# Hybrid decoder block: value products of four heads or more in one run, rotary sums on GpSimd, weight casts on ScalarE

## The chip, the cores and the metric

The kernel runs on one core of one Trainium2 chip. The metric is the device time of one execution in microseconds (us), the median of several runs. Shorter is better.

## The reference

One decoder layer over 512 tokens of width 1024, in float32. What matters here is its first part:

```python
h = rmsnorm(x, norm_mix_g); proj = h @ w_in                 # one projection for both head groups
# group A (8 heads): rotary queries, latent keys/values, an indexer picks 128 keys per query
index = einsum('bhqs,bqh->bqs', relu(qi @ ki), wi);  sel = top_k(causal(index), 128)
p = softmax(where(sel, s_A * 96**-0.5, -inf));       o_a = (p @ c_kv) @ w_uv
# group B (8 heads): three dilated causal patterns, merged by their softmax denominators
o_b = merge(dilated_attention(rope(q), rope(k), v))
x = x + concat(o_a, o_b) @ w_out
# then: cross-attention to 256 memory tokens, squared-ReLU MLP of width 4096, final RMSNorm
```

The kernel evaluates the dilated merge as one softmax with a bias (the logarithm of how often a key is seen), and the gathered top-k attention as a dense one whose unselected keys get a bias of -1e30.

## The kernel before, in words

**Dense products.** A weight is streamed in units of two K chunks (128 rows x 512 columns each): a DMA on SP's queue into a `wraw` buffer (three of them), a cast to float32r `whi`, and `wlo = wraw - whi` (six buffers each). A product is three matmuls per K chunk: hi x hi, hi x lo, lo x hi (`mm3`, L155). `split_unit` (L123) takes a letter for each unit: `p` casts on ScalarE and subtracts on GpSimd, `v` casts on ScalarE and subtracts on VectorE, capitals cast on VectorE instead.

**Rotary embedding.** `rope` (L256) reads a product from PSUM: four VectorE products with cosine, sine and minus sine (L271), then two VectorE sums (L279) into a token-row tile (`tok`, or `ghi2`/`ghi3` for the indexer's queries). TensorE transposes that tile (`tp<-ident,tok`). The sine half goes to a scratch tile `rb` with two buffers.

**Attention.** `attend` (L378) handles one block of 128 queries and the 8 heads of a group; there are four blocks in each of group B and group A, block b having 128(b+1) keys. Per head (two at once in the small blocks): a score product `sc`; one VectorE instruction (L407) that adds the bias and takes the row's extreme; an exponential on ScalarE with the row's sum (L409); a reciprocal (L410) and a VectorE product that normalises the row (L412); transposes of the 128x128 pieces into `tp`; a copy to `pT` (L420 on VectorE for two thirds of group A, L422 on ScalarE otherwise); then b+1 value products into `pv`, where even heads take PSUM partitions 0 to 63 (the left half of TensorE's columns) and odd heads 64 to 127 (the right half). The outputs of all heads are split into hi (ScalarE) and lo (VectorE) by `split_from` (L198), the left side of the output projection.

**Order.** The program is written as stages (`group_b(0)`, `queries_a(0)`, `top_k(1)`, `group_b(1)`, and so on, ending with four `group_a` blocks and `keys_cross`), and a scheduler then fixes the order of the instructions on each engine's queue; each queue runs strictly in that order. Filler for TensorE during attention are other products: the queries of group A, the cross-attention's keys (`mm<-h,whi`, 128x256), the first ones of the output projection. From the output projection on the order is the one written.

**Memory tokens.** `norm_mem` (L462) loads two tiles of memory rows into the buffers `ghi1` and `glo1`, squares them on ScalarE (L187), scales them on GpSimd (L467) and transposes them.

Of the kernel before, what the change touches and what calls it, by code (L numbers as in the profile page):

```python
# [11 lines left out]
F32 = mybir.dt.float32  # L12
# [5 lines left out]
P = 128  # L18
# [23 lines left out]
CONST_COLS = 512 + 128 + 3 * 128 + 3 * 64  # L42


def shape_constants():
    """Tables that depend on positions alone: group B's log-multiplicity bias, the causal
    bias of a diagonal block, and the rotary cosines and sines."""
# [7 lines left out]
    for d in (64, 32):  # L55
        inv = np.float32(10000.0) ** (-np.arange(0, d, 2, dtype=np.float32) / np.float32(d))
        ang = np.arange(S, dtype=np.float32)[:, None] * inv.astype(np.float32)[None, :]
        for tab in (np.cos(ang), np.sin(ang), -np.sin(ang)):
            tab = tab.astype(np.float32).reshape(NT, P, d // 2).transpose(1, 0, 2)
            cols.append(tab.reshape(P, NT * (d // 2)))  # L60
# [4 lines left out]
def kernel(  # L65
# [40 lines left out]
    def mmul(*a, **k):  # L106
        ins = nc.tensor.matmul(*a, **k)  # L107
        if ordered[0]:
            tc.keep_in_program_order(ins)

# [12 lines left out]
    def split_unit(raw, hi, lo, how="v"):  # L123
        """float32r hi and lo of raw; how names the engines: p the lo on GpSimd, v on VectorE,
        their capitals the hi on VectorE instead of ScalarE."""
# [6 lines left out]
    def load_weight(w, segs, k0, how, between=None):  # L132
        """w [rows, cols] in DRAM; the column segments side by side, K chunks k0..k0+7.
        Returns (hi, lo): lists over the K chunks of [128, ncols] views."""
# [20 lines left out]
    def mm3(dst, a, b, first=True, last=True, ks=None):  # L155
        """dst += sum_k a_k^T b_k, a and b as (hi list, lo list); lo x lo is below float32."""
# [6 lines left out]
    # ---- RMS norms: the gain is applied where the rows are transposed; a row's 1/rms is kept  # L163
    # apart and applied where the row's products come back ----
# [19 lines left out]
    def mean_square(src, junk, n=D, scale=None):  # L184
        """Mean of a row's squares over n columns, as this part of it adds to it."""
# [16 lines left out]
    def transpose_half(rows, g0, his, los, bank=bank_tp):  # L202
        """rows [128 tokens, 4 chunks of 128] -> transposed, times the gain, as hi + lo per chunk."""
# [11 lines left out]
    # =============================== token mixing ===============================  # L215
# [17 lines left out]
    tab64 = [tabs[:, 128 * i:128 + 128 * i].rearrange("p (t f) -> p t f", t=NT) for i in range(3)]  # L233
    tab32 = [tabs[:, 384 + 64 * i:448 + 64 * i].rearrange("p (t f) -> p t f", t=NT) for i in range(3)]
# [21 lines left out]
    def rope(ps, heads, half, tabs, t, dst, dup=None):  # L256
        """ps [128, heads, 2, half] (token rows, before the norm's 1/rms) -> dst like it, rotated
        by the token's position."""
        cos, sin, nsin = (tab[:, t, None, :].to_broadcast([P, heads, half]) for tab in tabs)
        r = r_mix[:, t:t + 1]  # L260
        n = heads * 2 * half
        rb = tmp.tile([P, 512], F32, name=nm("rb"), tag="rb", bufs=2)
        rbv = rb[:, :n].rearrange("p (h c f) -> p h c f", h=heads, c=2)
        if dup is None:
            ra = dst
        else:
            ra = tmp.tile([P, 512], F32, name=nm("ra"), tag="tok", bufs=2)[:, :n].rearrange(
                "p (h c f) -> p h c f", h=heads, c=2)
# [4 lines left out]
        for c in range(2):  # L273
            times(ra[:, :, c, :], ps[:, :, c, :], cos)
        times(rbv[:, :, 0, :], ps[:, :, 1, :], nsin)
        times(rbv[:, :, 1, :], ps[:, :, 0, :], sin)
        if dup is None:
            for c in range(2):
# [564 lines left out]
```

## Time and profile before

| what | value |
|---|---|
| runs (3) | 845.13, 845.95, 847.27 us; median 845.95 |
| the profiled execution, first to last instruction | 843.6 us |
| TensorE (PE) | busy 821.7 us, 97% |
| VectorE (DVE) / ScalarE (ACT) / GpSimd (POOL) | 474.4 / 331.4 / 293.2 us, 56 / 39 / 35% |
| mean granted TensorE clock | 0.992 |

The profiled execution has no time of its own beyond its span of 843.6 us; the median of the runs is 2.35 us above that, which is what lies around the span. The page cuts the span into 40 slices of 21 us and gives each engine's busy share; a busy TensorE is not one at its peak, since the intervals of its matmuls overlap and their ends are modelled. What a kind of matmul costs is read from one start to the next.

### The profile page before, as it was taken

The numbers are of one execution on the slowest core, as the hardware profiler recorded it, in microseconds if no ns is written. First come the engines' busy times: TensorE is split into PE (matmuls) and PEld (weight loads), VectorE is DVE, ScalarE is ACT, GpSimd is POOL, SyncE is SP. The second block draws the span as 40 slices with busy tenths as digits, with TensorE's granted clock in tenths as the row PEclk, the third lists the DMA queues.
The fourth block names the chain that finished last, engine by engine and source line by source line (L and its number), as shares of the span: only waits on it lengthen the run. The fifth ranks groups of instructions, "written<-read, shape, count | busy, mean of one in ns | idle before, by whom it ended". The sixth has DMA issues, their size and how long they took to land.

```text
span 843.6 us, 11086 instructions
## 1 busy us (share of the span) xinstructions
PE 821.7 (97%) x4182; PEld 679.2 (81%) x4182; DVE 474.4 (56%) x1010; ACT 331.4 (39%) x676; POOL 293.2 (35%) x179
## 2 busy tenths in 40 slices
PE   7899999999999999999999999999999999999997
PEld 6788787886787788788898878888888888888886
DVE  7876999998777634535673344423542244225413
ACT  5354424457754524223464433213431243123322
POOL 5734303131513405544501233333333333333351
PEclk9899999999999999999999999999999999999999
DMA  7443122112412303332510223333233322322202
GB/s 278 125 125 88 33 74 70 63 21 80 150 53 99 96 5 100 99 100 86 184 56 19 82 100 101 101 99 100 100 100 99 100 100 97 103 91 85 99 1 100
DMA packets 44516, 77.34 MB, mean 92 GB/s; under 512 B 4752, under 2 KB 10544, under 8 KB 44464
## 3 DMA queue, kind: packets, MB, share of 16 engines
q1 hardware_dynamic: 44464, 76.64, 27.8%
q8 instruction: 33, 0.54, 0.3%
q14 instruction: 19, 0.16, 0.1%
HBM read 74.01 MB, written 2.10 MB: 90 GB/s over the span
## 4 chain that ended last, share of the span: by engine, by line
PE 85%; DVE 11%; issue 1%; POOL 1%; ACT 1%; DMA 0%; SPq 0%; POOLq 0%; ACTq 0%; DVEq 0%
PE mm L107 71%; PE tp L112 5%; PE sc L107 5%; PE pv L107 4%; DVE m L525 1%; DVE ghi L360 1%; DVE tok L279 1%; DVE glo L526 1%; DVE rb L271 1%; DVE tok L271 1%; DVE whi L127 1%; DVE wlo L130 1%; DVE ghi L526 1%; DMA u2a<-in_x_dram 0%; DVE ghi L358 0%
## 5 line engine op out<-in xcount | busy, mean ns | idle before, releaser
L130 POOL TENSOR_TENSOR wlo<-wraw,whi 128x1024 fp32r<-128x1024 f32 (+2 forms) x107 | 256.2, 2408 | 404.5 <-ACT whi L129 318.8
L107 PE MATMUL mm<-whi,h 128*128 128x512 f32 (+2 forms) x624 | 200.1, 381 | 3.9 <-DVE h L213 2.0
L129 ACT CAST whi<-wraw 128x1024 fp32r<-128x1024 f32 (+3 forms) x111 | 114.3, 1030 | 149.6 <-PE mm L107 105.4
L107 PE MATMUL mm<-h,whi 128*128 128x512 f32 (+1 forms) x448 | 154.9, 369 | 0.0
L107 PE MATMUL mm<-wlo,h 128*128 128x512 f32 (+2 forms) x376 | 141.9, 379 | 0.2 <-DVE wlo L130 0.2
L107 PEld LDWEIGHTS mm<-whi,h 128*128 128x128 f32 x624 | 117.9, 195 | 22.0 <-ACT whi L129 2.2
L107 PE MATMUL mm<-u,whi 128*128 128x512 f32 x320 | 124.7, 390 | 0.0
L107 PE MATMUL mm<-u,wlo 128*128 128x512 f32 x320 | 123.5, 389 | 0.0
L107 PE MATMUL mm<-whi,ghi 128*128 128x512 f32 (+1 forms) x264 | 102.0, 390 | 0.0
L107 PE MATMUL mm<-whi,glo 128*128 128x512 f32 (+1 forms) x264 | 101.5, 385 | 0.0
L107 PE MATMUL mm<-wlo,ghi 128*128 128x512 f32 (+1 forms) x264 | 100.7, 383 | 0.0
L107 PEld LDWEIGHTS mm<-h,whi 128*128 128x128 f32 x448 | 81.1, 188 | 14.3 <-issue 1.0
L130 DVE TENSOR_TENSOR wlo<-wraw,whi 128x1024 fp32r<-128x1024 f32 (+2 forms) x24 | 62.2, 2591 | 37.5 <-ACT whi L129 37.5
L107 PEld LDWEIGHTS mm<-wlo,h 128*128 128x128 f32 x376 | 72.6, 194 | 11.1 <-DVE wlo L130 0.6
L107 PEld LDWEIGHTS mm<-u,whi 128*128 128x128 f32 x320 | 60.1, 188 | 12.4
L107 PEld LDWEIGHTS mm<-u,wlo 128*128 128x128 f32 x320 | 60.0, 188 | 12.5
L802 DVE TENSOR_TENSOR sq<-r 128x512 f32<-128x512 f32 x32 | 22.0, 689 | 66.7 <-ACT r L800 66.7
L107 PEld LDWEIGHTS mm<-whi,glo 128*128 128x128 f32 x264 | 49.6, 188 | 10.1 <-issue 0.2
L107 PEld LDWEIGHTS mm<-wlo,ghi 128*128 128x128 f32 x264 | 49.7, 188 | 9.6 <-issue 0.4
L107 PEld LDWEIGHTS mm<-whi,ghi 128*128 128x128 f32 x264 | 49.6, 188 | 9.4 <-issue 0.2
L409 ACT ACTIVATE p<-p,mx 128x128 f32<-128x128 f32 (+3 forms) x64 | 35.8, 560 | 29.4 <-DVE mx L407 28.5
L800 ACT ACTIVATE r<-mm 128x512 f32<-128x512 f32 x32 | 19.1, 598 | 64.8 <-PE mm L107 64.8
(212 smaller groups left out, 1116.7 us busy)
## 6 DMA issues: line engine op xcount, KB each, us to landing
wraw<-in_w_up_dram SPq DMA_DIRECT2D x32, 512.0 KB, 3.8
wraw<-in_w_down_dram SPq DMA_DIRECT2D x32, 512.0 KB, 3.6
wraw<-in_w_in_dram SPq DMA_DIRECT2D x16, 512.0 KB, 3.6
wraw<-in_w_kv_cross_dram SPq DMA_DIRECT2D x16, 512.0 KB, 3.9
wraw<-in_w_out_dram SPq DMA_DIRECT2D x8, 512.0 KB, 3.6
wraw<-in_w_q_cross_dram SPq DMA_DIRECT2D x8, 512.0 KB, 3.6
wraw<-in_w_o_cross_dram SPq DMA_DIRECT2D x8, 512.0 KB, 4.1
wraw<-in_w_in_dram SPq DMA_DIRECT2D x8, 256.0 KB, 2.9
```

The lines of the kernel that those rows point to most:

```text
L107: ins = nc.tensor.matmul(*a, **k)
L112: ins = nc.tensor.transpose(*a, **k)
L127: nc.vector.tensor_copy(hi, raw)
L129: nc.scalar.copy(hi, raw)
L130: (nc.gpsimd if how in "pP" else nc.vector).tensor_tensor(lo, raw, f32(hi), op=ALU.subtract)
L271: nc.vector.scalar_tensor_tensor(o, i, r, tab, op0=ALU.mult, op1=ALU.mult)
L279: nc.vector.tensor_tensor(dst[:, :, c, :], ra[:, :, c, :], rbv[:, :, c, :], op=ALU.add)
L360: nc.vector.scalar_tensor_tensor(acc[b], rl[:, :n], wh, acc[b], op0=ALU.mult, op1=ALU.add)
L409: nc.scalar.activation(pr[:, c], pr[:, c], AF.Exp, bias=mx[:, i:i + 1], scale=-1.0, accum_out=sm[:, i:i + 1])
L526: nc.vector.match_replace(acc[b], m8, acc[b], GONE)
L800: nc.scalar.activation(r, ps, AF.Relu)
L802: nc.vector.tensor_tensor(sq, r, r, op=ALU.mult)
```

## The change

Four things are done together.

- **`attend`.** Heads are taken in pairs (2j, 2j+1), several pairs at once in the small blocks. The exponentials are not normalised; their sums are gathered in one tile of 8 columns. The value products wait until four heads or more are transposed and copied, and then run together, key chunk by key chunk, alternately for the even and the odd head of a pair, in an order held by hand. After the last: one reciprocal, a GpSimd copy that spreads it over 512 columns (`rx`), four transposes, a ScalarE copy (`rT`), one VectorE product with `pv` (`o`), the hi cast on ScalarE and the lo on GpSimd, both now from SBUF. All `pT` copies are on ScalarE; `pT` has five buffers.
- **`rope`.** The cosine table is doubled, so there are three VectorE products and one sum of full width, on GpSimd except for the small key ropes. The scratch is one tile of the buffer `ghi1`, its halves in turn.
- **Casts.** The indexer queries' weights, group B's value weights and the cross-attention's key weights go from `PPPP`, `vpvp` and `PPpp` to `pppp`.
- **Buffers.** `sel` is BF16; the residual rows 2 and 3 are loaded into a pool that opens after attention's pool has closed.

The core of the diff:

```diff
@@ constants: four tables of 128 and of 64 columns
-        for tab in (np.cos(ang), np.sin(ang), -np.sin(ang)):
+        for tab in (np.tile(np.cos(ang), (1, 2)), np.sin(ang), -np.sin(ang)):
...
@@ rope
+    rbs = mtile([P, 2, 512], F32, "ghi1")
+    turn = [0]
+    def rope(ps, heads, half, tabs, t, dst, add=nc.gpsimd):
...
-        rb = tmp.tile([P, 512], F32, name=nm("rb"), tag="rb", bufs=2)
+        rbv = rbs[:, turn[0], :heads * 2 * half].rearrange("p (h c f) -> p h c f", h=heads, c=2)
...
-        for c in range(2):
-            times(ra[:, :, c, :], ps[:, :, c, :], cos)
+        times(dst.rearrange("p h c f -> p h (c f)"), ps.rearrange("p h c f -> p h (c f)"),
+              cos[:, t, None, :].to_broadcast([P, heads, 2 * half]))
         times(rbv[:, :, 0, :], ps[:, :, 1, :], nsin)
         times(rbv[:, :, 1, :], ps[:, :, 0, :], sin)
-            for c in range(2):
-                nc.vector.tensor_tensor(dst[:, :, c, :], ra[:, :, c, :], rbv[:, :, c, :], op=ALU.add)
+        add.tensor_tensor(dst, dst, rbv, op=ALU.add)
...
-    wb = load_weight(w_in0, [(C_QI, C_QI + 512)], 0, "PPPP")
+    wb = load_weight(w_in0, [(C_QI, C_QI + 512)], 0, "pppp")
...
-    wv = load_weight(w_in0, [(C_VB, C_VB + 512)], 0, "vpvp")
+    wv = load_weight(w_in0, [(C_VB, C_VB + 512)], 0, "pppp")
...
@@ attend
-        per = 2 if b == 0 or b == 1 and chunk0 else 1
+        per = max(1, 512 // n) if b != 2 else 1
+        sums = main.tile([P, NH], F32, name=nm("sums"), tag="sums", bufs=2)
+        ready, last = [], None
+        for j0 in range(0, NH // 2, per):
...
-            nc.vector.reciprocal(rc, sm)
-            for i, (h, c) in enumerate(hs):
-                nc.vector.tensor_scalar(pr[:, c], pr[:, c], rc[:, i:i + 1], None, op0=ALU.mult)
...
-            if chunk0 == 0 and g % 3 != 1:
-                nc.vector.tensor_copy(pT[:, :m], tp[:, :m])
-            else:
-                nc.scalar.copy(pT[:, :m], tp[:, :m])
+                both = nc.scalar.copy(pT[:, :per * n], tp[:, :per * n])
...
+            if len(ready) < 2:
+                continue
+            for j, pair in ready:
                 for kc in range(b + 1):
+                    for i in range(2):
+                        ins = mmul(pvv[i * DH:(i + 1) * DH, j, :], vtile[kc // 2][:, kc % 2, h * DH:(h + 1) * DH],
+                                   pair[i][:, kc * P:(kc + 1) * P], start=kc == 0, stop=kc == b)
...   (each waits for the last copy of its run and stands behind the product before it)
+        nc.vector.reciprocal(rc, sums)
+        rx = att.tile([P, 512], F32, name=nm("rx"), tag="p", bufs=3)
+        nc.gpsimd.tensor_copy(rx.rearrange("p (h f) -> p h f", f=DH), rc[:, :, None].to_broadcast([P, NH, DH]))
+        tp = bank_tp()
+        for j in range(4):
+            tpose(tp[:, j * P:(j + 1) * P], rx[:, j * P:(j + 1) * P], ident)
+        rT = att.tile([P, 512], F32, name=nm("rT"), tag="pT", bufs=5)
+        nc.scalar.copy(rT, tp)
+        o = att.tile([P, 512], F32, name=nm("o"), tag="p", bufs=3)
+        nc.vector.tensor_tensor(ov, pvv, rT.rearrange("p (j t) -> p j t", t=P), op=ALU.mult)
...
-            split_from(pvv[:, 2 * i:2 * i + 2, :], heads_hi[q][:, :, bsl], heads_lo[q][:, :, bsl])
+            nc.scalar.copy(hi, part)
+            nc.gpsimd.tensor_tensor(heads_lo[q][:, :, bsl], part, f32(hi), op=ALU.subtract)
...
-        sel[b] = att.tile([P, n], F32, name=f"sel{b}")
+        sel[b] = att.tile([P, n], BF16, name=f"sel{b}")
...
-        wt = load_weight(w_kv[0], [(512 * i, 512 * i + 512)], 0, "PPpp")
+        wt = load_weight(w_kv[0], [(512 * i, 512 * i + 512)], 0, "pppp")
...
-    xr = [mtile([P, D], F32, f"u3{'ab'[t]}") if t < 2 else res.tile([P, D], F32, name=f"xr{t}") for t in range(NT)]
+    p1b.close()
+    p2 = ctx.enter_context(tc.tile_pool(name="tmp2", bufs=1, reuse_waits="tile"))
+    xr = [mtile([P, D], F32, f"u3{'ab'[t]}") if t < 2 else p2.tile([P, D], F32, name=f"xr{t}") for t in range(NT)]
```

TensorE's queue where group B's block 2 begins, before: `pv` are value products, one row a head and value tile (`u3a`, `u3b`), `tp` transposes of probabilities `p`, `sc` scores, `mm<-ident,glo` transposes of memory rows.

```order
L112 MATMUL tp_2059<-ident,p_2051 128x128 x3
L112 MATMUL mm_2020<-ident,glo_396_2010 128x128 x2
L112 MATMUL tp_2078<-ident,p_2070 128x128 x3
L107 MATMUL sc_2144<-u2b_1115,u2a_934 128x384
L107 MATMUL pv_2048<-pT_2063,u3a_804 64x128 x2
L107 MATMUL pv_2048<-pT_2063,u3b_805 64x128
L112 MATMUL tp_2097<-ident,p_2089 128x128 x3
L112 MATMUL mm_2021<-ident,glo_396_2010 128x128 x2
L107 MATMUL pv_2048<-pT_2082,u3a_804 64x128 x2
L107 MATMUL pv_2048<-pT_2082,u3b_805 64x128
L107 MATMUL sc_2163<-u2b_1115,u2a_934 128x384
```

And in the changed kernel:

```order
L107 MATMUL mm_1830<-whi_1713,h_12_108 128x384
L107 MATMUL sc_1946<-u2b_1071,u2a_902 128x384
L107 MATMUL sc_1947<-u2b_1071,u2a_902 128x384
L113 MATMUL tp_1824<-ident,tok_1818 96x128 x4
L113 MATMUL tp_1861<-ident,tok_1855 96x128 x4
L107 MATMUL sc_1970<-u2b_1071,u2a_902 128x384
L107 MATMUL sc_1971<-u2b_1071,u2a_902 128x384
L113 MATMUL tp_1958<-ident,p_1950 128x128 x3
L107 MATMUL sc_2006<-u2b_1071,u2a_902 128x384
L113 MATMUL tp_1964<-ident,p_1951 128x128 x3
L113 MATMUL tp_1982<-ident,p_1974 128x128 x3
L107 MATMUL sc_2007<-u2b_1071,u2a_902 128x384
```

The value products no longer follow each head; they come eight rows further down as one run of twelve for four heads, `pT` of the even and the odd head in turn. After the first row shown, the last product of group A's queries, TensorE has only scores and transposes left until the first exponentials are done.

ScalarE's queue at the same place of the changed kernel (`ghi_347` and `glo_356` are the memory rows, `tok` a rotary query's tile, `p` exponentials):

```order
L468 ACTIVATE tok_1855<-mm_1830,r_mix 128x4x64
L475 COPY u_217_1240<-tp_1824 96x4x128
L475 COPY u_217_1240<-tp_1861 96x4x128
L188 ACTIVATE junk_1870,ss_1872<-ghi_347_1868 128x1024
L188 ACTIVATE junk_1908,ss_1910<-glo_356_1906 128x1024
L406 ACTIVATE p_1950,sums_1945<-p_1950,mx_371_1952 128x384
L406 ACTIVATE p_1951,sums_1945<-p_1951,mx_372_1953 128x384
```

The squares of the memory rows stand ahead of block 2's exponentials. On SP's queue the load of `ghi` stood right behind that of `bias`, ahead of all of attention; it is now behind the last rotary sum, since it takes the buffer that holds `rope`'s scratch:

```order
L146 DMA wraw_2833<-in_w_kv_cross_dram 128x2x512
L531 DMA h_419_2104<-krT 32x8x512
L481 DMA ghi_347_1868<-in_mem_dram 128x1024
L146 DMA wraw_2839<-in_w_kv_cross_dram 128x2x512
L146 DMA wraw_2845<-in_w_kv_cross_dram 128x2x512
```

GpSimd's queue of the changed kernel during group B's query and key projections, where `tok_*` at L275 are the rotary sums:

```order
L131 TENSOR_TENSOR wlo_1074<-wraw_1072,whi_1073 128x1024
L131 TENSOR_TENSOR wlo_1080<-wraw_1078,whi_1079 128x1024
L275 TENSOR_TENSOR tok_952<-tok_952,ghi_37_238 128x512
L275 TENSOR_TENSOR tok_988<-tok_988,ghi_37_238 128x512
L275 TENSOR_TENSOR tok_1024<-tok_1024,ghi_37_238 128x512
L131 TENSOR_TENSOR wlo_1086<-wraw_1084,whi_1085 128x1024
L131 TENSOR_TENSOR wlo_1092<-wraw_1090,whi_1091 128x1024
L131 TENSOR_TENSOR wlo_1318<-wraw_1316,whi_1317 128x768
L275 TENSOR_TENSOR tok_1060<-tok_1060,ghi_37_238 128x512
```

Before, this queue held only the `wlo` rows; a rotary sum now stands behind up to three of them.

## Rows read from the trace of the kernel before

**Rows 1.** The page's list of busy times: engine, busy us (share of the span) xinstructions.

```profile
PE 821.7 (97%) x4182; PEld 679.2 (81%) x4182; DVE 474.4 (56%) x1010; ACT 331.4 (39%) x676; POOL 293.2 (35%) x179
```

**Rows 2.** The page's chain of work that ended last, by engine.

```profile
PE 85%; DVE 11%; issue 1%; POOL 1%; ACT 1%; DMA 0%; SPq 0%; POOLq 0%; ACTq 0%; DVEq 0%
```

**Rows 3.** The view of waits, TensorE's: engine, line, what it waited for; us in total, times, the longest.

```profile
PE tp L112 <- DVE tok L279: 3.8, 2, 2.0
...
PE tp L112 <- DVE h L213: 2.1, 3, 1.0
PE mm L107 <- DVE h L213: 2.0, 1, 2.0
```

**Rows 4.** Busy time of each engine in six stretches that cover the span: start-up; the projections and the indexer; group B's blocks 0 and 1 with group A's queries; blocks 2 and 3 of group B, the memory rows, group A's keys; the end of group B's last block and group A; the rest from the output projection on. Columns: the stretch, its length, then busy us (xinstructions) of PE, PEld, DVE, ACT and POOL, the granted clock, the DMA engines' share and GB/s.

```profile
0.00:31.40 31.40, 22.25 (x125) 20.05 (x126) 25.79 (x69) 15.44 (x43) 19.80 (x27) 0.89 0.68 232
31.40:132.50 101.10, 99.07 (x463) 81.37 (x462) 85.27 (x217) 39.92 (x71) 36.05 (x20) 0.98 0.27 80
132.50:186.00 53.50, 51.67 (x331) 46.17 (x330) 52.94 (x181) 24.97 (x68) 14.97 (x11) 1.00 0.17 51
186.00:226.40 40.40, 40.18 (x223) 25.46 (x221) 34.11 (x101) 30.67 (x78) 13.20 (x6) 1.00 0.38 118
226.40:307.30 80.90, 80.90 (x569) 65.33 (x568) 51.12 (x156) 38.98 (x104) 20.84 (x9) 1.00 0.22 72
307.30:843.60 536.30, 527.63 (x2480) 440.82 (x2478) 225.21 (x288) 181.38 (x317) 188.34 (x109) 1.00 0.27 91
```

**Rows 5.** The same view, same columns, of two short stretches, and of the 100 us in which VectorE is fullest.

```profile
24.50:31.30 6.80, 5.96 (x28) 5.95 (x29) 6.80 (x23) 2.86 (x9) 5.12 (x5) 0.50 0.43 123
106.40:109.80 3.40, 3.40 (x10) 2.75 (x9) 3.37 (x8) 1.11 (x2) 1.11 (x1) 0.50 0.74 193
80.00:180.00 100.00, 96.14 (x514) 81.58 (x513) 98.73 (x296) 39.39 (x88) 28.18 (x17) 0.98 0.21 60
```

**Rows 6.** The same view of the instructions on `pv` alone (columns PE, PEld, DVE, ACT, clock, DMA share, GB/s).

```profile
132.50:186.00 53.50, 6.36 (x48) 4.67 (x48) 1.63 (x4) 1.50 (x4) 1.00 0.17 51
186.00:226.40 40.40, 11.52 (x80) 8.38 (x80) 0.84 (x2) 0.74 (x2) 1.00 0.38 118
226.40:307.30 80.90, 21.56 (x192) 16.50 (x192) 3.34 (x8) 3.33 (x9) 1.00 0.22 72
```

**Rows 7.** Timeline of TensorE, two places: the value products of one head of a 512-key block with the score product behind them, and the first and the last of eight neighbours where a run of one head and a run of a head of the other column half adjoin. Columns: start us, duration us, engine, line, operation, out<-in, shapes, xcount.

```profile
213.17 0.65 PE L107 MATMUL pv<-pT,u3a 128*64 128x128 f32 x4
213.66 0.60 PE L107 MATMUL pv<-pT,u3b 128*64 128x128 f32 x4
214.19 1.12 PE L107 MATMUL sc<-u2b,u2a 64*128 64x512 f32 x2
...
293.98 0.27 PE L107 MATMUL pv<-pT,vAb 128*64 128x128 f32 x1
...
294.37 0.27 PE L107 MATMUL pv<-pT,vAa 128*64 128x128 f32 x1
```

**Rows 8.** Timeline of all engines around 103 us, and a pair of rotary sums at a quiet place; in brackets the idle time before the instruction and what ended it.

```profile
98.64 8.87 POOL L130 TENSOR_TENSOR wlo<-wraw,whi 128x1024 fp32r<-128x1024 f32 x4 [16.35 <-ACT whi L129]
...
103.21 2.62 DVE L279 TENSOR_TENSOR tok<-tok,rb 128x256 f32<-128x256 f32 x2
...
105.97 0.70 PE L112 MATMUL tp<-ident,tok 128*128 128x128 f32 x4 [1.95 <-DVE tok L279]
...
120.69 0.74 DVE L279 TENSOR_TENSOR tok<-tok,rb 128x256 f32<-128x256 f32 x2
```

**Rows 9.** Groups of instructions on VectorE: line, operation, out<-in, shapes, xcount; busy us, mean ns of one; idle us before it and what ended it.

```profile
L412 DVE TENSOR_SCALAR p<-p,rc 128x128 f32<-128x128 f32 (+3 forms) x64 | 33.0, 532 | 1.1
L127 DVE CAST whi<-wraw 128x1024 fp32r<-128x1024 f32 x20 | 27.0, 1353 | 4.9 <-DMA wraw<-in_w_q_cross_dram 2.1 <-PE mm L107 2.0 <-POOL r_cross L182 0.7
L279 DVE TENSOR_TENSOR tok<-tok,rb 128x256 f32<-128x256 f32 (+1 forms) x32 | 14.4, 485 | 0.0
L420 DVE COPY pT<-tp 128x256 f32<-128x256 f32 (+2 forms) x18 | 9.5, 531 | 6.9 <-PE tp L112 5.8 <-PE pv L107 0.7
L200 DVE TENSOR_TENSOR glo<-pv,ghi 128x256 fp32r<-128x256 f32 x16 | 6.6, 415 | 2.3 <-ACT ghi L199 2.3
```

**Rows 10.** The same of GpSimd: a weight's lo, a memory tile's scaling, and a product of two 128x512 tiles from the kernel's end.

```profile
L130 POOL TENSOR_TENSOR wlo<-wraw,whi 128x1024 fp32r<-128x1024 f32 x98 | 239.0, 2452 | 363.1 <-ACT whi L129 277.4 <-DVE whi L127 60.8 <-PE mm L107 23.6
L467 POOL TENSOR_SCALAR glo<-glo,rmem 128x1024 f32<-128x1024 f32 x1 | 2.9, 2870 | 0.1
L770 POOL TENSOR_TENSOR xr<-xr,g_fin 128x512 f32<-128x512 f32 x2 | 2.6, 1294 | 0.2
```

**Rows 11.** The same of ScalarE: a weight's cast, the copy of a 128x512 `pT`, the square of a memory tile, the hi cast of a block's outputs.

```profile
L129 ACT CAST whi<-wraw 128x1024 fp32r<-128x1024 f32 x100 | 105.1, 1051 | 139.6 <-PE mm L107 99.8 <-DMA wraw<-in_w_up_dram 22.6 <-issue 6.1
L422 ACT COPY pT<-tp 128x512 f32<-128x512 f32 x15 | 8.8, 584 | 15.0 <-PE tp L112 14.1 <-PE pv L107 0.9
L187 ACT ACTIVATE junk<-glo 128x1024 bf16<-128x1024 f32 x1 | 1.1, 1059 | 0.0
L199 ACT CAST ghi<-pv 128x256 fp32r<-128x256 f32 x16 | 6.0, 372 | 9.2 <-PE pv L107 8.7 <-DVE glo L200 0.5
```

**Rows 12.** The view of DMA issues: out<-in, queue, xcount, KB each, median us from issue to landing.

```profile
ghi<-in_mem_dram SPq DMA_DIRECT2D x1, 512.0 KB, 6.3
glo<-in_mem_dram SPq DMA_DIRECT2D x1, 512.0 KB, 3.3
```

## Prediction made before the changed kernel ran

> **What bounds the kernel now.** I read the busy times first: TensorE is busy 97% of the span, every other engine 56% or less [rows 1]. The chain of waits agrees: 85% of it is TensorE, 11% VectorE [rows 2]. So a change pays only where it shortens what TensorE does, or takes away a time in which TensorE waits; work taken from VectorE is worth nothing by itself. The view of waits shows how little waiting there is: 3.8 us for the rotary tile `tok` in two pieces, and 4.1 us for the transposed rows `h` at the start [rows 3]. The table by stages then says where each can be won [rows 4]. Group B and group A, from 132.5 to 307.3 us, hold all value products that the page counts, 39.4 us in 320 instructions [rows 6], 0.123 us each. From 307.3 us on nothing is edited but the loads of two residual rows; I put that stage at 0, within 2 us either way.
>
> The profiled span is 843.6 us; the median of the runs, 845.95, is 2.35 above it. I sum against the span and add the 2.35 at the end.
>
> **Value products.** Eight of one head stand in one column half and take 1.02 us to the start of the next product, 0.13 each. Where runs of the two halves adjoin, eight starts follow each other within 0.39 us: seven steps of 0.056 [rows 7]. So two halves in turn do work side by side, and the change makes all of them do so. 320 x 0.056 = 17.9 us; for the ends of the 14 runs that are left I add one product of the slow kind each, 14 x 0.13 = 1.8 (an estimate). That is 19.7 in place of 39.4. By stage, with the same counts [rows 6]: 6.4 becomes 3.1 (-3.3), 11.5 becomes 4.9 (-6.6), 21.6 becomes 11.8 (-9.8).
>
> **The spread sums.** Each of eight blocks adds four transposes. Four took 0.70 us with the last one's own 0.27 in it [rows 8, 7], so about 0.45 for the queue: +3.6, of which 0.9, 0.9 and 1.8 in the three stages. Around them stand a reciprocal, a copy on GpSimd, a copy on ScalarE and a product on VectorE. The trace has no such GpSimd copy; the nearest row is a product of two 128x512 tiles, 1.29 us [rows 10], and from nothing to twice that is my bound.
>
> **Work off VectorE.** Gone are 33.0 us of normalising products, 9.5 of copies, 6.6 of output lo parts, and most of the rotary sums [rows 9]. VectorE is busy 98.7 of the 100 us from 80 to 180 [rows 5], so there it matters, through the two waits for `tok`. The longer look at one: the pair of sums took 2.62 us in place of 0.74, in a time when GpSimd ran four `wlo` without a break, and the transposes behind it waited 1.95 [rows 8]. After that wait the granted clock is 0.50, the 1.2 GHz level, for 3.4 us [rows 5], which gives back 1.7 if it stays at 2.4 GHz. With the sums on GpSimd that block can't occur in this form: -1.95 - 1.7 = -3.65 in the stage up to 132.5. The second wait, 3.8 - 2.0 = 1.8, lies in the next stage.
>
> What is late next is the sum itself: 1.29 us on GpSimd behind up to three `wlo` of at most 2.45 [rows 10]. Before its transposes TensorE has the next token tile's 24 products, some 4.5 us at the 96.14 us for 514 instructions of that time [rows 5], which covers nearly two of those. I take it as covered; if not, see the third rival.
>
> **Start-up.** The 4.1 us for `h` [rows 3] end on VectorE, and 1.35 us casts [rows 9] and some small rotary instructions leave its queue. Half of it gone is my figure: -2.0. The bounds are 0, and -7.5 if the waits and the 6.8 us at half clock behind them [rows 5] go entirely.
>
> **Group B's first blocks** (132.5 to 186): -1.8 - 3.3 + 0.9 = -4.2.
>
> **Group B's other blocks** (186 to 226.4). TensorE's need falls from 40.2 [rows 4] by 6.6 - 0.9 to 34.5 us. But the memory rows now come late: they are loaded into rotary scratch, so after the last rotary sum, while before the load had landed long ago. From the last query product: VectorE's three products 0.7 and the sum 1.2 (estimates), the landing 3.3 to 6.3, I take 4.8 [rows 12], two squares of 1.06 [rows 11] that stand ahead of the first exponential: 8.8 us. By the order TensorE has four score products by then, each at most the 1.05 us of a 512-key one [rows 7], and some transposes: about 4 us, so it waits some 5. Behind that ScalarE is the bound. It was busy 30.7 us in this stage [rows 4]; the squares (2.5 with their read-outs), two `rT` copies (2 x 0.58) and two casts (2 x 1.05) [rows 11] make it 36.5. Without the squares and the two casts, which can wait, 31.9 follow the 8.8: 40.7 against 40.4 before. I add 1.2 for gaps: +1.5, so the 5.7 us that TensorE saves here are lost. The bounds are -5.7 and +4.
>
> That is where a page speaks against the change. The Trainium skill, "TensorEngine Tiling (Array Packing)", PSUM Bottleneck, says that side-by-side tiles speed up TensorE but not the emptying of PSUM, and advises to use ScalarE and VectorE both for it; here all `pT` copies go to ScalarE. By that rule the stage gains nothing, as in my sum; without it the sum would be 7 us lower.
>
> **Group A** (226.4 to 307.3). -9.8 + 1.8 = -8.0 for TensorE. Against it: the output lo parts on GpSimd stand behind two `wlo` of 2.45 [rows 10] at its start, and the tile `o` holds one of three buffers for probabilities meanwhile, so I put 3.6 us of waiting there. At its end the filler products are used up: the blocks 2 and 3 stand bare, and their tail (spread, transposes, `rT`, `o`, hi 2 x 0.37, lo) is about 5 us long, half of it covered by the first tiles of the output projection: 2.5. Together -1.9, from -6 to +4.
>
> **Sum.** -2.0 - 3.65 - 4.2 + 1.5 - 1.9 = -10.25: a span of 833.4, and with 2.35 a time of 836 us. About 0.3% (2.5 us) is what a measurement of this kernel can tell from no change.
>
> **The rivals.**
> - *No new wait takes anything.* The load lands early enough and the buffers suffice: TensorE keeps all of -19.7 + 3.6, and the waits of 3.65 and 1.8 go. -21.5: 824.5. For it: in the trace ScalarE is busy 39% overall [rows 1]. Against it: 36.5 us of ScalarE work in a stage that TensorE could do in 34.5. Chance 0.14.
> - *The halves gain less in long runs.* If the steps of 0.056 hold only at the seams and a run in turn goes at 0.11, the products keep 37 us: 836 + 17 less the idle time that this fills (about 10): 843. Against it: seven equal steps in a row [rows 7]. Chance 0.07.
> - *The rotary sums wait on GpSimd instead.* A sum and a `wlo` that stands in its way trade places: the 3.65 + 1.8 us stay, at other tiles. 841.5. The row speaks for it: a VectorE sum of two tiles stood still until GpSimd's `wlo` was done [rows 8]. In the Trainium skill, "SBUF — State Buffer", Who interferes with whom, a VectorE instruction with two SBUF inputs and a GpSimd one that reads SBUF exclude each other for a whole instruction; the trace agrees (2.62 against 0.74). With more than 35 us of work added on GpSimd, the indexer's sums on VectorE would meet it more often. Chance 0.16.
> - *Slower: TensorE falls to its lower clock in the bare stretches.* Twice in the trace the clock is at 1.2 GHz after TensorE waited some 2 us [rows 3, 5]. The change makes a wait of 5 us for the memory rows, and leaves group A's last two blocks without filler, some 27 us (a third of that stage's 80.9 [rows 4], an estimate), in which waits come between short runs. Work done at the lower level takes twice as long, so each us of it costs one. It decides at 12.7 us of such work: then the sum is above +2.5. With 15 us, 851. Against it: a clock of 1.00 in all stages after 132.5 [rows 4]. Chance 0.13.
>
> **Numbers.** The forecast has 0.50 and its own range is 831 to 841. Eight in ten lie between 825 and 847: from the first rival up to a part of the last. Faster by over 0.3% are the forecast, the first and most of the third rival, some of the second: 0.74; within 0.3%: 0.12; slower: 0.14.
>
> **What would show it.** In the changed profile: value products at about 0.056 us from start to start, 14 runs; no wait of TensorE for `tok`, and a clock of 1.00 around 100 us; a wait of about 5 us for exponentials of block 2, with ScalarE behind the memory rows' load; the stage from there to group A as long as before; waits of about 6 us in group A. I am wrong if group B's later blocks get shorter by over 4 us, if TensorE waits for rotary tiles, or if the stage after 307 us moves by over 2.

## The result: 857.96 us, 1.4% slower

| kernel | median of the runs, us | ratio to the kernel before (95%) |
|---|---|---|
| before | 845.88 | |
| changed | 857.96 (856.99 to 859.36) | 1.0137 (1.012 to 1.0155) |

The forecast was 836, with a range of 825 to 847: wrong in sign. (With a fourth run of 845.82 us the kernel before has a median of 845.88 in place of 845.95.) The profiled execution of the changed kernel spans 857.6 us, against 843.6. Its page, busy times first:

```profile
PE 818.7 (95%) x4214; PEld 675.8 (79%) x4214; DVE 411.4 (48%) x793; ACT 346.1 (40%) x702; POOL 328.9 (38%) x224
...
PEclk9899999995999999999999999999999999999999
```

VectorE lost 63 us of work, as intended, and TensorE 3 us [rows 1], but TensorE now idles longer, and one slice of 21 us, the tenth, has the clock at 0.5. The view of waits, TensorE's, answers to [rows 3]:

```profile
PE sc L107 <- DVE mx L404: 7.5, 3, 5.6
PE tp L113 <- POOL tok L275: 5.6, 4, 2.6
PE tp L113 <- DVE h L214: 4.3, 3, 3.2
...
PE mm L107 <- ACT whi L130: 2.7, 1, 2.7
```

The wait for rotary tiles did not go; it moved from VectorE (3.8 us in two) to GpSimd (5.6 in four), and there is a new one of 5.6 us, in front of scores. The times below are starts of work that all kernels share, read from their timelines: the first 512-column product, the last product of group A's queries, the first one of the cross-attention's queries, the end. They cut the span into four parts:

| us | start-up | to the last query product | to the cross-attention | rest |
|---|---|---|---|---|
| before | 31.5 | 154.1 | 159.8 | 498.2 |
| changed | 34.1 | 156.0 | 167.3 | 500.2 |
| forecast, change | -2.0 | -7.85 | -0.4 | 0 |
| measured, change | +2.6 | +2.0 | +7.5 | +2.0 |

**The third part.** Timeline of the changed kernel behind the last query product, columns as in [rows 7] with the idle time before in brackets:

```profile
191.98 0.45 POOL L275 TENSOR_TENSOR tok<-tok,ghi 128x128 f32<-128x128 f32 x1 [1.71 <-PE tp L113]
...
192.46 0.35 SPq L481 DMA_DIRECT2D ghi<-in_mem_dram  x1
...
193.06 0.91 PE L107 MATMUL sc<-u2b,u2a 64*128 64x384 f32 x2
197.80 1.06 ACT L188 ACTIVATE junk<-ghi 128x1024 bf16<-128x1024 f32 x1 [4.05 <-DMA ghi<-in_mem_dram]
...
198.85 1.04 ACT L188 ACTIVATE junk<-glo 128x1024 bf16<-128x1024 f32 x1
198.98 0.56 DVE L404 CUSTOM_DVE_ANT_0 p<-sc,bias 128x384 f32<-128x384 f32 x1 [6.70 <-ACT junk L188]
...
199.60 1.65 PE L107 MATMUL sc<-u2b,u2a 64*128 64x384 f32 x2 [5.63 <-DVE mx L404]
199.89 0.60 ACT L406 ACTIVATE p<-p,mx 128x384 f32<-128x384 f32 x1
```

This is the chain of the forecast up to the squares: the last rotary sum, then the load, then the squares, and the first exponential 9.5 us after the last product (8.8 was said). TensorE's own wait ends before that exponential, by a link that the forecast did not have. The next scores need a PSUM bank that VectorE empties (L404); VectorE had stood idle 6.70 us until ScalarE's first square was done, because the squares' unused output `junk` takes two of the three buffers of the probabilities `p` that VectorE writes (line 482 of the changed kernel, tag `p`). What was not in the sum stands in the score products' own durations: 0.91 us for two before the wait, 1.65 for two behind it. The table of stretches (columns as in [rows 4]) shows why:

```profile
195.00:200.00 5.00, 0.40 (x1) 0.40 (x2) 0.57 (x2) 2.20 (x5) 0.80 (x2) 0.56 0.27 98
200.00:204.00 4.00, 4.00 (x9) 1.52 (x9) 1.13 (x4) 2.97 (x9) 3.72 (x4) 0.50 0.00 0
204.00:208.00 4.00, 4.00 (x15) 2.59 (x14) 1.38 (x5) 2.20 (x6) 2.79 (x1) 0.50 0.00 0
208.00:212.00 4.00, 4.00 (x11) 1.90 (x9) 1.80 (x7) 2.47 (x10) 0.00 (x0) 0.50 0.01 4
212.00:216.00 4.00, 4.00 (x29) 2.95 (x28) 1.03 (x4) 1.30 (x5) 0.00 (x0) 0.50 0.01 2
216.00:220.00 4.00, 4.00 (x20) 2.15 (x18) 1.40 (x4) 2.33 (x7) 0.61 (x1) 0.99 0.00 0
```

For 20 us, from 196 to 216, the granted clock is 0.50, the 1.2 GHz level, though from 200 us on TensorE is busy all the time, with scores and transposes. It rises after two runs of twelve value products (from 212.7 to 215.5 us). ScalarE, which the forecast took for the bound here, is busy about half the time.

**The first two parts.** VectorE and GpSimd at one of the new waits:

```profile
106.74 7.07 POOL L131 TENSOR_TENSOR wlo<-wraw,whi 128x1024 fp32r<-128x1024 f32 x3
...
107.08 2.47 DVE L352 SCALAR_TENSOR_TENSOR ghi<-rl,weff,ghi 128x384 f32<-128x384 f32 x1
...
109.87 2.23 DVE L350 TENSOR_SCALAR ghi<-rl,weff 128x512 f32<-128x512 f32 x1
112.02 1.93 DVE L353 TENSOR_TENSOR ghi<-ghi,bias 128x128 f32<-128x128 f32 x1
...
115.19 0.73 DVE L269 SCALAR_TENSOR_TENSOR tok<-mm,r_mix,tabs 128x512 f32<-128x512 f32 x1
...
116.85 1.26 POOL L275 TENSOR_TENSOR tok<-tok,ghi 128x512 f32<-128x512 f32 x1 [3.05 <-DVE ghi L269]
...
118.16 0.66 PE L113 MATMUL tp<-ident,tok 128*128 128x128 f32 x4 [2.17 <-POOL tok L275]
```

GpSimd runs three subtractions in a row, which end at about 109.1, 111.8 and 113.8 us. Three of the indexer's instructions on VectorE, which work from SBUF to SBUF, each end 0.1 to 0.5 us behind one of these: at 109.55, 112.10 and 113.95. The rotary products behind them on VectorE's queue start late, the sum later still, while GpSimd itself stood idle for 3.05 us in front of it. So the view of waits names GpSimd, but the lateness is VectorE's. This wait left the clock at 1.00; the longest one did not:

```profile
126.48 0.66 PE L113 MATMUL tp<-ident,tok 128*128 128x128 f32 x4 [2.64 <-POOL tok L275]
...
127.00:131.00 4.00, 4.00 (x13) 3.15 (x12) 3.90 (x9) 1.07 (x2) 0.00 (x0) 0.57 0.00 0
```

### The profile page after: what moved, and what is told of

Its sections match the earlier page's. It is cut to its first block, busy times and chain, and to the rows that moved or that the text cites. A ratio compares the mean times of both kernels' runs of the same rounds, so it can differ in the third digit from the quotient of the medians.

```text
span 857.6 us, 11040 instructions
## 1 busy us (share of the span) xinstructions
PE 818.7 (95%) x4214; PEld 675.8 (79%) x4214; DVE 411.4 (48%) x793; ACT 346.1 (40%) x702; POOL 328.9 (38%) x224
## 4 chain that ended last, share of the span: by engine, by line
PE 82%; DVE 9%; issue 3%; POOL 2%; DMA 2%; ACT 2%; POOLq 0%; SPq 0%; ACTq 0%; DVEq 0%
PE mm L107 69%; PE sc L107 5%; PE tp L113 5%; PE pv L107 2%; POOL wlo L131 1%; DVE ghi L352 1%; DMA wraw<-in_w_o_cross_dram 1%; DVE whi L128 1%; DVE m L543 1%; DVE glo L544 1%; DVE ghi L269 1%; DMA ghi<-in_mem_dram 1%; ACT whi L130 0%; DVE kk L275 0%; DVE wlo L131 0%
## 5 line engine op out<-in xcount | busy, mean ns | idle before, releaser
L131 POOL TENSOR_TENSOR wlo<-wraw,whi 128x1024 fp32r<-128x1024 f32 (+2 forms) x109 | 260.3, 2403 | 282.8 <-ACT whi L130 252.4
L130 ACT CAST whi<-wraw 128x1024 fp32r<-128x1024 f32 (+3 forms) x119 | 122.1, 1030 | 158.0 <-PE mm L107 100.5
L107 PE MATMUL mm<-h,whi 128*128 128x512 f32 (+1 forms) x448 | 149.7, 361 | 0.0
L107 PEld LDWEIGHTS mm<-whi,h 128*128 128x128 f32 x624 | 118.2, 195 | 22.3 <-ACT whi L130 3.1
L131 DVE TENSOR_TENSOR wlo<-wraw,whi 128x1024 fp32r<-128x1024 f32 (+2 forms) x22 | 58.8, 2672 | 40.5 <-ACT whi L130 40.5
L107 PEld LDWEIGHTS mm<-u,wlo 128*128 128x128 f32 x320 | 60.1, 188 | 12.5
L107 PEld LDWEIGHTS mm<-whi,ghi 128*128 128x128 f32 x264 | 50.0, 189 | 11.2 <-ACT ghi L451 1.5
```

What stands on the lines that cost most here:

```text
L130: nc.scalar.copy(hi, raw)
L131: (nc.gpsimd if how in "pP" else nc.vector).tensor_tensor(lo, raw, f32(hi), op=ALU.subtract)
```

## Experiments

The experiments are numbered E1 to E12. The scheduler fixes the queues anew for each kernel, so an edit can also change the order of other work. Of the 1594 matmuls ahead of the cross-attention that are not value products, the traces show 25 out of sequence in E1 and 191 in E3, both against the changed kernel, and 2 in E6 and 74 in E10, both against E5. So E1 and E6 are nearly free of that side effect, and the others are not.

**Late load and fall of the clock.** E1 gives the rotary sums of group A's queries a scratch of their own; all queues keep nearly the same order:

```diff
+    rqs = tmp.tile([P, 2, 128], F32, name="rqs")
...
-        rbv = rbs[:, turn[0], :heads * 2 * half].rearrange("p (h c f) -> p h c f", h=heads, c=2)
+        rbv = (rqs if heads == 4 else rbs)[:, turn[0], :heads * 2 * half].rearrange("p (h c f) -> p h c f", h=heads, c=2)
```

> The changed kernel, except that the rotary sums of group A's queries use a small scratch of their own (2 x 128 columns), so that the memory rows' load no longer waits for the last of them. The other queues keep nearly the same order. Theory L (late load): the load at 192.5 us makes TensorE wait 5.6 us and then leaves it at 1.2 GHz for 20 us, in which it was busy 16.6 us, so some 8 us of work at full speed are lost: together about 13. Expected 844 to 847, no wait over 1 us in front of group B's block 2, clock 1.00 there. Rival S (ScalarE bounds the stage anyway, as forecast): the wait is spread over the exponentials instead, and the time is 853 or more.

Measured: 845.42 us, 0.9992 of before (0.9978 to 1.0006), 12.5 less than the changed kernel. The load is issued at 147.5 us in place of 192.5. Of the 5.63 us wait 0.65 is left, and the same stage runs at full clock. The first row below is the load's issue (its durations in ns, then its first and last start), the second the stage:

```profile
L482 SPq DMA_DIRECT2D ghi<-in_mem_dram x1: 341/341/341, 147.5 to 147.5; - x1
...
190.00:212.00 22.00, 20.41 (x131) 12.16 (x131) 12.26 (x42) 16.55 (x47) 4.84 (x6) 1.00 0.15 31
```

Theory L holds in size and place; S falls.

E4 does the opposite: of the change, only the scratch in `ghi1`, put into the kernel before.

```diff
+    rbs = mtile([P, 2, 512], F32, "ghi1")
+    turn = [0]
...
-        rb = tmp.tile([P, 512], F32, name=nm("rb"), tag="rb", bufs=2)
-        rbv = rb[:, :n].rearrange("p (h c f) -> p h c f", h=heads, c=2)
+        turn[0] ^= 1
+        rbv = rbs[:, turn[0], :n].rearrange("p (h c f) -> p h c f", h=heads, c=2)
```

> The kernel before with one part of the change alone: rotary scratch in the buffer ghi1, so that the memory rows load after the last rotary sum. Theory L: the same wait and fall of the clock as in the changed kernel, 8 to 13 us, so 854 to 859. Rival: before, TensorE has other products to fill the wait and the load is hidden: 846 to 849.

Measured: 860.04 us, 1.0165 of before (1.015 to 1.018). TensorE waits 5.92 us at the same place and the clock is at 0.50 for 10 us. The wait and half of those 10 us are some 11 us of the 13.8; start-up is 1.4 longer as well. One buffer name is enough for a loss of the changed kernel's size, without any other part of the change.

E11 keeps the load late and fills the wait:

```diff
             nc.scalar.copy(qA[:, 4 * g:4 * g + 4, t * P:(t + 1) * P], tp[0:96])
+        if g == 1:
+            fill = bank_mm()
+            mm3(fill[:, :384], h_tok(0), wt)
```

> The changed kernel, with 24 products of 128x384 more on TensorE (one token tile of the queries' projection over again, its result unused) in front of the scores that wait for the memory rows; the load is as late as before. They take 4.2 us at full speed and fill the wait. If the fall of the clock behind that wait is what costs, the stage runs at 1.00 and the time is 848 to 851, in spite of more work. If the wait itself (5.6 us) and ScalarE's late start are the cost, 857 to 859, since nothing after the load comes earlier. If ScalarE then bounds the stage in spite of a full clock, 853 to 857.

Measured: 852.44 us, 5.5 less than the changed kernel, with more work on TensorE. The load is still issued at 191.9 us; the wait and the 20 us at 0.50 are gone, but a wait of 1.43 us at 215.9 us is followed by some 7 us at 0.50:

```profile
190.00:220.00 30.00, 27.48 (x166) 17.55 (x165) 14.05 (x46) 22.59 (x60) 13.82 (x12) 0.98 0.25 70
```

The time lies between the first case and the third. So holding the clock up is worth 5.5 us with a load that is as late, and some 3.5 more (half of the 7 at 0.50) were lost again. From the other side: of E1's 12.5 us, 5.0 are the wait (5.63 less 0.65), and 7.5 are left for the clock.

**The casts.** E3 sets the three weights' letters back:

```diff
-    wb = load_weight(w_in0, [(C_QI, C_QI + 512)], 0, "pppp")
+    wb = load_weight(w_in0, [(C_QI, C_QI + 512)], 0, "PPPP")
...
-    wv = load_weight(w_in0, [(C_VB, C_VB + 512)], 0, "pppp")
+    wv = load_weight(w_in0, [(C_VB, C_VB + 512)], 0, "vpvp")
...
-        wt = load_weight(w_kv[0], [(512 * i, 512 * i + 512)], 0, "pppp")
+        wt = load_weight(w_kv[0], [(512 * i, 512 * i + 512)], 0, "PPpp")
```

> The changed kernel with the casts of the three weights as before (PPPP, vpvp, PPpp); everything else as changed. If the casts on ScalarE and the two subtractions more on GpSimd are what makes the start and the stage up to 140 us longer (8 us later there than before), 850 to 854. If they are harmless, 857 to 859.

Measured: 842.13 us, 0.9962 of before (0.9939 to 0.9985): 15.8 less than the changed kernel, with the late load still in it (a wait of 5.28 us, and 0.50 for some 13 us only). That is more than either case allowed.

E8 puts only the moved casts into the kernel before:

```diff
-    wb = load_weight(w_in0, [(C_QI, C_QI + 512)], 0, "PPPP")
+    wb = load_weight(w_in0, [(C_QI, C_QI + 512)], 0, "pppp")
...
-    wv = load_weight(w_in0, [(C_VB, C_VB + 512)], 0, "vpvp")
+    wv = load_weight(w_in0, [(C_VB, C_VB + 512)], 0, "pppp")
...
-        wt = load_weight(w_kv[0], [(512 * i, 512 * i + 512)], 0, "PPpp")
+        wt = load_weight(w_kv[0], [(512 * i, 512 * i + 512)], 0, "pppp")
```

> The kernel before with one part of the change alone: the three weights' casts as in the changed kernel. If these casts cost by themselves, 850 to 858 (third experiment: 15.8 us). If they cost only together with rotary sums on GpSimd, which then has both, 845 to 848.

Measured: 859.05 us, 1.015 of before (1.0135 to 1.0165). So moving the casts costs by itself, about 13 us, without rotary sums on GpSimd. Of these, 2.5 lie in the start-up and 4.8 in the part up to the last query product. Another 5.5 lie in the third part, where TensorE is busy for 164.1 us in place of 159.6 with as many matmuls (971) and a clock of 1.00. That points at their order, not at a cast; no run tests it.

E5 undoes the late load and the casts (the two diffs of E1 and E3):

> The changed kernel with both repairs: memory rows loaded early (own small scratch for the queries' sums) and the three casts as before. If the late load (12.5 us by the first experiment) and the casts (15.8 by the third) are separate terms, they add: 829 to 832. If the earlier start had only hidden part of the late load's cost, less: 834 to 840.

Measured: 834.47 us, 0.9861 of before (0.9847 to 0.9876). Against E1 the casts cost 10.9. If the two gains simply added (857.96 - 12.5 - 15.8) the time would be 829.6, so some 5 us overlap, as E3's shorter time at 0.50 suggests.

E7 has the early load and only the indexer's cast back, E10 is E5 with only the value weights' casts moved:

```diff
 E7, against E1
-    wb = load_weight(..., 0, "pppp")
+    wb = load_weight(..., 0, "PPPP")
 E10, against E5
-    wv = load_weight(..., 0, "vpvp")
+    wv = load_weight(..., 0, "pppp")
```

> The changed kernel with the memory rows loaded early (845.4 in the first call) and only the indexer queries' weights cast on VectorE as before; the value weights and the cross keys stay as changed. If the start-up is where the casts cost (ScalarE's queue has the transposed rows then), about 3 to 5 us are gained: 840 to 842. If the two subtractions of the value weights on GpSimd block VectorE's indexer sums, nothing is gained here: 844 to 847. Both: 835 to 840.

> As the kernel of 834.5 us, but with the value weights' casts as changed (pppp: two subtractions of 2.45 us more on GpSimd, two of VectorE's gone). The indexer's cast alone accounted for 2.6 of the 10.9 us that the casts cost. Theory B (VectorE's indexer sums are blocked by back-to-back subtractions on GpSimd): this cast holds most of the other 8.3: 840 to 843. If it is the cross keys' cast instead: 833 to 836.

Measured: E7 842.79 us, so the indexer's cast is worth 2.6 of the 10.9. E10 841.53, so moving two subtractions from VectorE to GpSimd costs 7.1. Both times are where theory B put them; its mechanism holds only in part, as shown below. TensorE's waits for rotary tiles up to 145 us, E5 and then E10:

```profile
PE tp L113 <- POOL tok L276: 1.1, 1, 1.1
```

```profile
PE tp L113 <- POOL tok L276: 5.9, 4, 2.9
```

Up to the last query product E10 takes 9.1 us longer (156.05 against 146.96). TensorE's waits there are 5.5 longer (4.8 for rotary tiles, 0.7 for `weff`), and behind two of them it is at 0.50 for 6.8 us, worth half, 3.4. The indexer's sums on VectorE, the same seven instructions each, E5 and then E10:

```profile
L353 DVE SCALAR_TENSOR_TENSOR ghi<-rl,weff,ghi 128x384 f32<-128x384 f32 x7 | 5.5, 789 | 0.0
L353 DVE SCALAR_TENSOR_TENSOR glo<-rl,weff,glo 128x256 f32<-128x256 f32 x7 | 3.4, 485 | 7.6 <-ACT rl L348 7.5
```

```profile
L353 DVE SCALAR_TENSOR_TENSOR glo<-rl,weff,glo 128x256 f32<-128x256 f32 x7 | 8.8, 1263 | 7.3 <-ACT rl L348 7.1
L353 DVE SCALAR_TENSOR_TENSOR ghi<-rl,weff,ghi 128x384 f32<-128x384 f32 x7 | 7.8, 1118 | 0.0
```

The 256-column sum takes 1.26 us on average in place of 0.49, and the two groups grow by 7.7, more than the two subtractions took on VectorE (2.6 each in the kernel before). But the subtractions that these sums meet are not the moved ones. The indexer's first score product, the sums at issue and GpSimd's subtractions, E5 and then E10:

```profile
54.76 0.48 PE L107 MATMUL sc<-glo,u 128*128 128x256 f32 x2
...
72.24 0.48 DVE L353 SCALAR_TENSOR_TENSOR glo<-rl,weff,glo 128x256 f32<-128x256 f32 x1 [1.13 <-ACT rl L348]
73.22 9.93 POOL L131 TENSOR_TENSOR wlo<-wraw,whi 128x1024 fp32r<-128x1024 f32 x4 [15.87 <-ACT whi L130]
```

```profile
60.50 0.40 PE L107 MATMUL sc<-glo,u 128*128 128x256 f32 x2
...
72.45 10.03 POOL L131 TENSOR_TENSOR wlo<-wraw,whi 128x1024 fp32r<-128x1024 f32 x4 [14.19 <-ACT whi L130]
72.69 2.45 DVE L353 SCALAR_TENSOR_TENSOR glo<-rl,weff,glo 128x256 f32<-128x256 f32 x1 [1.55 <-ACT rl L348]
75.67 4.56 DVE L353 SCALAR_TENSOR_TENSOR glo<-rl,weff,glo 128x256 f32<-128x256 f32 x2 [0.53 <-ACT rl L348]
```

Both kernels have four subtractions of the next weights at that place. In E5 the 256-column sums are over by then. In E10 the indexer starts 5.7 us later, and its last three sums stand still beside them. Two things make it late. The value weights' four subtractions now run without a break (47.4 to 57.0 us), and the indexer's third rotary sum comes behind them, at 56.98 in place of 53.70. And TensorE transposes the first indexer tile at 53.44 in place of 48.52, though its sum was done at 46.0 and TensorE did not wait: that is the scheduler's order. How much of the 7.1 is each is open; a run with the order held fixed would tell. What remains of the 10.9 us for the cross keys' cast, 1.2, is within what these runs tell apart.

**Rotary sums.** E2 is the changed kernel with them on VectorE, E9 is E5 with them there:

```diff
-    def rope(ps, heads, half, tabs, t, dst, add=nc.gpsimd):
+    def rope(ps, heads, half, tabs, t, dst, add=nc.vector):
```

> The changed kernel with all rotary sums on VectorE; everything else as changed, the late load too. Theory G (GpSimd): the waits for rotary tiles of 2.2 and 2.6 us and the clock fall behind them belong to sums that stand behind VectorE's late products on a third engine; without them 3 to 5 us are gained: 853 to 855. Rival V: VectorE's instructions are what GpSimd's weight subtractions block, so the sums only change engine and the waits stay: 857 to 860.

> Memory rows early, casts as before (834.5 in the second call) and all rotary sums on VectorE: of the change the new attention alone is left, with three rotary products in place of four. In the first call the sums on VectorE gained 3.7 us, with the casts moved. If GpSimd is the wrong place for them in any case, 831 to 833. If they were only in the way of the moved casts' subtractions, VectorE's sums are blocked by GpSimd's subtractions as they were in the kernel before: 835 to 840.

Measured: E2 854.21 us, 3.7 less than the changed kernel, theory G's figure, though one wait of 1.95 us for a rotary tile is left, V's mechanism. E9 836.12 us, 1.65 more than E5, V's figure. So the place of the sums depends on the casts: with them moved, the sums are better on VectorE; with them as before, GpSimd is no worse, and 1.65 is less than the 2.5 us that the forecast took as the least that shows. E9's waits up to 145 us have this line:

```profile
PE tp L113 <- DVE tok L276: 1.0, 3, 0.7
```

With the casts as before, the waits of 3.8 us for rotary tiles go on either engine (1.1 in E5), so it is not the move to GpSimd that removes them.

**Value products.** E6 is E5 with the even head's key chunks first in a run, then the odd head's; the other instructions keep their places:

```diff
-                for kc in range(b + 1):
-                    for i in range(2):
+                for i in range(2):
+                    for kc in range(b + 1):
```

> As the run before, except that inside a run of value products the even head's key chunks come first and the odd head's after them, not in turn; the other rows of all queues stay in their places. Forecast's price: 320 products at 0.056 us in turn against 0.11 to 0.13 in one half, 17 to 20 us more on a TensorE that is busy throughout: 845 to 850. Rival: ScalarE or VectorE bounds the attention stages, and the products only fill its waits: within 4 us of the run before.

Measured: 837.45 us, 3.0 more than E5. The forecast's price for the order falls. The rival's figure is met, but not for its reason: the products themselves differ by no more than that. Stretches of the instructions on `pv` alone, columns as in [rows 6], E5 and then E6:

```profile
130.00:230.00 100.00, 10.28 (x160) 8.59 (x160) 2.75 (x4) 1.00 0.29 86
```

```profile
130.00:230.00 100.00, 12.12 (x160) 10.43 (x160) 2.75 (x4) 1.00 0.27 83
```

Group A's half reads alike, so all 320 take 20.6 us in E5 and 24.2 in E6, against 39.4 before. The step from 39.4 to 24.2 is there without the order in turn. Gathering four heads explains it, though no run gathers them and leaves the rest of the new attention out: written head after head, the heads of the two halves still run beside each other. A piece of E6's timeline shows it. The even head's chunks, first two from `vAa`, then two from `vAb`, stand in the order ahead of all of the odd head's, whose first two come from `vAa`:

```profile
288.36 0.65 PE L107 MATMUL pv<-pT,vAa 128*64 128x128 f32 x4
288.85 0.27 PE L107 MATMUL pv<-pT,vAb 128*64 128x128 f32 x1
288.85 0.32 PE L107 MATMUL pv<-pT,vAa 128*64 128x128 f32 x1
288.96 0.27 PE L107 MATMUL pv<-pT,vAb 128*64 128x128 f32 x1
289.01 0.27 PE L107 MATMUL pv<-pT,vAa 128*64 128x128 f32 x1
```

The even head's `vAb` and the odd head's `vAa` start in turn, as they already did in [rows 7], where I read the seam as a pattern that only an order in turn extends.

**ScalarE as the bound.** E12 is E5 with the odd heads' `pT` copies on VectorE:

```diff
-                both = nc.scalar.copy(pT[:, :per * n], tp[:, :per * n])
+                both = (nc.scalar.copy if i == 0 else nc.vector.tensor_copy)(pT[:, :per * n], tp[:, :per * n])
```

> As the kernel of 834.5 us, with the copies of the odd heads' transposed probabilities on VectorE, the even heads' on ScalarE. If ScalarE bounds group B's later blocks (30.7 us busy of 40 there), as forecast, 3 to 6 us are gained: 828 to 832. If TensorE does (37.6 of 40), nothing: 833 to 836.

Measured: 832.94 us, 0.9848 of before (0.9834 to 0.9863), the fastest of all: 1.5 less than E5, just outside the second case. With the load early, ScalarE is not what bounds the stage; sharing the copies is a small gain.

## Why the prediction was wrong

- **Value products** (39.4 to 19.7): right in size, 20.6 in E5. The reason was half right: of the 18.8 us, the order in turn brings 3.6 (E6); the other 15.2 come without it, by the gathering of four heads as far as the traces tell.
- **The spread sums**: no sign of trouble. The GpSimd copy took 0.61 us (eight of them 4.9), below the row taken as nearest.
- **Work off VectorE** (-3.65, and -1.8 in the next part): this step failed. It priced the rotary sums leaving VectorE, and put at nothing, without a reason, what the moved casts add to GpSimd and ScalarE. They cost 10.9 us (E5 against E1), 7.1 of them by the value weights' two subtractions (E10): the indexer comes later, its sums on VectorE then stand still beside GpSimd's subtractions, and the rotary products behind them are late for TensorE. How much of that is the scheduler's new order is open. The row was there: a pair of sums of 2.62 us in place of 0.74 [rows 8]. The third rival used it, but took a swap at even cost. The Trainium skill, "SBUF — State Buffer", Who interferes with whom, says as much of VectorE instructions with two SBUF inputs. The two of the three above that have two agree (2.47 us, and 1.93 where the same shape took 0.27 in E10). The third, a scaling with a single tile as input, stood still too (2.23 us; 0.47 in E10 while GpSimd was idle). The Trainium skill, same section, allows for that, since it counts `tensor_scalar` among the instructions that can enter a two-port mode; no trace shows the mode.
- **Start-up** (-2.0): wrong in sign, +2.6. With the casts back it is 31.5 to 32.2 us (E3, E5), as before: so the other edits gain nothing there. E7 names the loss: with the indexer's cast back the first 512-column product starts at 31.1 us, in E1 at 34.0.
- **Group B's first blocks** (-4.2): about right once load and casts are undone; the second part is 7.1 us shorter in E5 than before, where the forecast had -7.85 for the two terms in it. The reason was not: with the sums on VectorE (E9) 5.5 of it are there as well.
- **Group B's other blocks** (+1.5, bounds -5.7 to +4): the second step that failed. The load's lateness and the wait of 5 us were right (5.6), its price wrong. The sum made ScalarE the cause of all that followed, and had nothing for the fall of the clock. That was left to a rival with chance 0.13, which named this wait but looked for most of the slow work in group A's bare stretches; those ran at 1.00. The clock fell behind the wait that the sum itself had, and stayed at 0.50 until 216 us. That is worth 5.5 (E11) to 7.5 us (E1) beside the 5.0 of the wait. The wait was more than twice as long as those of [rows 3] that were followed by 0.50 in [rows 5], so the fall belonged in the same term.
- **Group A** (-1.9): waiting there was put at 6.1 us and is 4.0 in the changed kernel, 1.47 the longest. The gain is smaller than that suggests. In E1, with the load early, TensorE's work in the third part falls by 11.2 us (159.6 to 148.4), where the two stages had 13.7, and the part is 5.3 shorter. The forecast's terms for it without the late load, -5.7 and -1.9, give 7.6.
- **The rest** (0): +2.0 in the changed kernel, +1.2 in E5, but only 0.1 and 0.2 in E4 and E8, which keep the old attention and buffers. Which of those edits it is was not looked for.

The two failed steps account for the difference: 12.5 us for the load and 10.9 for the casts take 857.96 to 834.47. That this is close to the forecast's 836 is partly luck. The 836 held a price for the late load (+1.5 in place of -5.7). Without it the same sum gives 829, which E5 missed by over 5 us, since start-up, group A and the rest gained less than forecast.

## What to carry to other kernels

When a scratch tile is given an idle buffer, look at who takes that buffer next: here the next owner was a load that the whole attention stage waits for. Price a wait of TensorE together with the work behind it at the lower clock; here the clock cost about as much as the wait, or more. Before moving SBUF-to-SBUF work from VectorE to GpSimd, count which VectorE instructions then meet GpSimd's work. Where a scheduler fixes the order, look also at what it moved.

## What the runs showed of the hardware

- After the wait of 5.6 us the granted clock stayed at 0.50 for 16 us in which TensorE is shown busy without a gap, with scores of 64 rows and 128x128 transposes; with much the same work and a wait of 0.65 us before it (E1) it was 1.00 throughout. It rose after runs of value products in both column halves. E4, with other products between, was at 0.50 for 10 us.
- Waits of about 2 us did not all have the same effect: after 2.64 us (at 126.5 us of the changed kernel) the clock was at 0.50 for some 4 us, after 2.17 us (at 118.2) it stayed at 1.00.
- Value products of opposite column halves overlap also when one head's stand wholly behind the other's: 0.076 us each (24.2 over 320) against 0.064 in turn (20.6), and 0.13 for one head alone [rows 7].
- A VectorE instruction with one SBUF tile as input (a scaling, 128x512) took 2.23 us beside GpSimd's subtractions, and 0.47 in E10 while GpSimd was idle.
